# Strassen pairs of a feed-forward projection collected in running PSUM banks, with VectorE making the weight and column sums

## The chip, the cores and the metric

The kernel runs on one core of one Trainium2 chip. Its engines are TensorE (PE in the profile, its weight loads PEld), VectorE (DVE), ScalarE (ACT), GpSimd (POOL) and SyncE (SP), which only issues transfers here. The metric is the device time of one execution in microseconds; less is better. Compared are medians of runs of the kernel before and of the changed one.

## The reference, cut to what matters

One step of a decoder layer for a prompt of 512 tokens and eight samples of one token: 520 columns in all. The change touches the last part, behind the mixing of the two attention branches:

```python
mix = sigmoid(ga) * (oa @ w_pa) + sigmoid(gb) * (ob @ w_pb)
h = x + mix @ w_o
f = square(relu(rmsnorm(h, g_norm2) @ w_up))      # w_up: 1024 x 4096
y = rmsnorm(h + f @ w_down)                       # w_down: 4096 x 1024
```

All of it is float32. The outputs are `y`, the new key and value caches and the recurrent states.

## The kernel before

Activations lie transposed in SBUF: 128 features on the partitions, 520 columns along the row, in eight tiles `k` for the 1024 features. The columns fall in two halves of 260 (`HC`); `halves` shows a tile that way.

A float32 product is made of three matmuls, since operands are rounded to a shorter format (`F32R`): the rounded part is `hi`, the remainder `lo`, and the sum is hi x hi + hi x lo + lo x hi. Weights are split so on the chip: `split_piece` has ScalarE round a piece of 128 x 512 (`whi`, L107) and VectorE subtract (`wlo`, L108). `weight_tiles` gives the buffers, four of each kind in one pool and a fifth from a second pool.

Weights come in panels of 128 output features x 1024 input features. `self.panels` lists them in order: `w_in`, `w_pa`, `w_pb`, eight of `w_o`, and then four quarters (`qd`) of the feed-forward part, each with eight panels of `w_up` and eight of `w_down`. Panel `i+2` is loaded and panel `i+1` split while panel `i` is multiplied.

In the first three quarters the `w_up` panels run as four pairs (`PAIR`), by Strassen's scheme: seven products P1 to P7 of half size in place of eight. Each is a group of 12 matmuls (four input tiles, three passes) into 260 columns, so a pair has 84. `load_pair` loads the two panels and, with an accumulating transfer from GpSimd's queue (L96), the sums of their blocks (`sums`). `pair_pieces` yields the seven weight pieces, of which two (`s2`, `s4`) are sums that GpSimd adds (L124, L125). `column_sums` makes the matching sums of the activations (`hg`, the normalised `h` before the norm's factor) into `Th` and `Tl`. P1, P2 and P3 take `hh` and `hl`, the others `Th` and `Tl`. P6 needs the sums of the lower four tiles.

`pair_mm` runs the seven groups into three PSUM places: `a` and `b`, the two banks of a tile `m` (two such tiles), and `c`, a bank of its own (`self.pf`, four banks). `up_pair` combines them behind each group: ScalarE copies P1 and P5 out (L1092), VectorE adds (L1098, L1100, L1105, L1106, L1108), and ScalarE takes relu and square and rounds the result `f` to `fh`; VectorE makes `fl`. These are what the `w_down` panels read, whose results collect in `dd` (`panel_mm`, L225).

`H` is `h`; while `w_o` runs (L1296 on), VectorE adds its panels to `H` (L1298), ScalarE makes `hh` and `hg`, `column_sums` follows for the same tile, and the squares of `H` are added into `acc` for the norm. `spread` sums `acc` over the partitions on TensorE (L1317) and takes the reciprocal into `rv` (L1320); it stands behind the first pair. `rv` is used in the fourth quarter.

The order of an engine's instructions comes from a scheduler, which orders them by its own timing; `high_priority` moves a block ahead, `behind` forces an order without a wait, `after` adds a wait. In the pairs `behind` holds the matmuls of one pair in turn, but groups of different pairs and panels may interleave. Each engine then runs its list strictly in turn, waiting on semaphores.

GpSimd's queue also holds copies of the old caches from memory to memory (`pace`, L267), each held back until a certain matmul of `self.last` has run.

Of the kernel before, what the change touches and what calls it, by code (L numbers as in the profile page):

```python
# [9 lines left out]
F32 = mybir.dt.float32  # L10
# [37 lines left out]
class Build:  # L48
# [42 lines left out]
    def load_pair(self, i):  # L91

        ap, p = self.panels[i][0], self.late
        sums = p.tile([P, KT, P], F32, tag="sums", name="sums", bufs=2)
# [16 lines left out]
    def weight_tiles(self, n):  # L111
        self.nw += 1
        pool, bufs = (self.late, 1) if self.late is not None and self.nw % 5 == 0 else (self.wp, self.wbufs)
        return [pool.tile([P, n, P], F32R, tag=t, name=t, bufs=bufs) for t in ("whi", "wlo")]

    def pair_pieces(self, i):

        nc = self.nc
        ra, rb, sums = self.raw.pop(i)
        new = lambda: self.late.tile([P, 4, P], F32, tag="s", name="s", bufs=3)  # L120
        yield self.split_piece(ra, 0, 4)
        yield self.split_piece(sums, 4, 4)
        s2, s4 = new(), new()
        nc.gpsimd.tensor_tensor(s2, sums[:, 4:], ra[:, :4], op=ALU.add)  # L124
        nc.gpsimd.tensor_tensor(s4, s2, ra[:, 4:], op=ALU.add)  # L125
        order = {"12": lambda: self.split_piece(ra, 4, 4), "s2": lambda: self.split_piece(s2, 0, 4),
                 "s4": lambda: self.split_piece(s4, 0, 4), "s3": lambda: self.split_piece(sums, 0, 4),
                 "22": lambda: self.split_piece(rb, 0, 4)}
        for n in (("12", "s2") if i in self.first_pairs else ("s2", "12")) + ("s4", "s3", "22"):
            yield order[n]()  # L130
# [39 lines left out]
    def pair_mm(self, acts, done):  # L170
# [3 lines left out]
        m, c = self.pm.tile([P, 2, 512], F32, tag="m", name="mps"), self.bank("mps")  # L174
        a, b = m[:, 0, :HC], m[:, 1, :HC]
        c = c[:, :HC]
        mid = (("P2", a, False), ("P6", b, True)) if i in self.first_pairs else (("P6", b, True), ("P2", a, False))
        prev = None
        for q, (n, o, fresh) in enumerate((("P1", a, True), ("P5", c, True), *mid, ("P3", c, False), ("P7", b, False),
                                           ("P4", a, True))):  # L180
            with self.tc.high_priority():
                self.pieces_to(i, q + AHEAD)
            if q == 4 and i + 2 < len(self.panels):
                self.load_panel(i + 2)
            hi, lo = self.ready[i][q]
            for k in range(4):
                xh, xl = acts(n, k)
                for x, (w, u) in enumerate(((hi, xh), (hi, xl), (lo, xh))):
                    mm = nc.tensor.matmul(o, w[:, k], u, start=(fresh and k == 0 and x == 0), stop=(k == 3 and x == 2),  # L189
                                          skip_group_check=True)  # L190
# [29 lines left out]
    def k_tile(self, out, w, kw, k, xh, xl, kt):  # L220

        for j in range(2):
            o = out[j] if isinstance(out, list) else out[:, j]
            for n, (wt, x) in enumerate(self.passes(w, kw, xh, xl)):
                self.last = self.nc.tensor.matmul(o[:, :HC], wt, x[:, k, j * HC:(j + 1) * HC],  # L225
                                                  start=(k == 0 and n == 0), stop=(k == kt - 1 and n == 2))
# [831 lines left out]
    def column_sums(self, p, b, k, hi, lo):  # L1058
# [5 lines left out]
        if k < 4:  # L1064
            ts = slice(0, 1)
            nc.gpsimd.tensor_tensor(t[:, 0], b11, b12, op=ALU.subtract)
        else:
            ts = slice(1, 4)
            e = nc.vector if k == KT - 1 else nc.gpsimd
            e.tensor_tensor(t[:, 0], b22, b12, op=ALU.subtract)  # L1070
# [6 lines left out]
    def up_pair(self, p, work, k, fh, fl):  # L1077

        nc, tc, t, v = self.nc, self.tc, [work(), work()], {}
        new = lambda n: p.tile([P, HC], F32, tag=n, name=n, bufs=2)  # L1080
        one, two = slice(0, HC), slice(HC, NT)

        def split(x):
            nc.scalar.activation(t[x], t[x], AF.Square)
            nc.scalar.activation(fh[:, k + x], t[x], AF.Copy)
# [479 lines left out]
```

## Time and profile before

| | us |
|---|---|
| runs of the kernel before, median of 3 | 913.65 |
| lowest and highest of them | 912.48, 916.57 |
| the profiled execution's own time | 913.32 |
| its span, first to last instruction | 911.5 |
| matmuls of `w_o`, last panel ends | at 528.96 |
| first quarter with its pairs begins | at 530.24 |
| last matmul of the third quarter | at 808.56 |

A row of the trace's list in time has the start from the span's beginning, the length, engine, line, operation, the tile written and those read, and in brackets the idle time before it with what ended it. In grouped rows `x` is a count, then come busy time and the mean nanoseconds of one, then idle time ahead. TensorE's lengths overlap: a matmul of 260 columns is shown 0.28 us long, and starts follow each other faster than that.

### The profile page before, as it was taken

What the parts mean: (1) busy time and instruction counts of PE and PEld (TensorE: products, weight loads), DVE (VectorE), ACT (ScalarE), POOL (GpSimd) and SP (SyncE); (2) the same over time, 40 slices, a digit from 0 to 9 for tenths busy, and PEclk for the clock granted to TensorE, in tenths of its full rate; (3) what the DMA queues carried; (4) which work ended last, traced back from release to release, by engine and by line L of the source; (5) the groups of instructions that cost most, each with busy time, mean ns of one, the idle gap of its engine ahead of it and who ended that gap; (6) DMA issues with size and microseconds to landing.
All of it is one profiled execution on the core that took longest, in us unless ns stands there. A gap on an engine that the chain in (4) does not pass through costs nothing. (4 is left out here: it accounts for less than half of the span.)

```text
span 911.5 us, 19609 instructions
## 1 busy us (share of the span) xinstructions
PE 888.3 (97%) x8010; PEld 868.0 (95%) x8010; DVE 596.2 (65%) x1172; ACT 417.7 (46%) x844; POOL 128.9 (14%) x170
## 2 busy tenths in 40 slices
PE   9999999999999999999999969999999999999996
PEld 9999999999999999999999969999999989999996
DVE  6866666865867678676655588644863476656634
ACT  6334324454654454457334457623852466224342
POOL 1200000000111112010001433014301330000000
PEclk9999999999999999999999989999999999999998
DMA  7466455324534642222797966698869862222302
GB/s 252 155 239 210 131 202 204 117 73 157 196 132 151 213 148 91 76 72 72 279 318 274 290 221 195 231 339 295 244 232 353 254 224 94 102 92 90 136 9 86
DMA packets 42721, 165.16 MB, mean 181 GB/s; under 512 B 5692, under 2 KB 10820, under 8 KB 40808
## 3 DMA queue, kind: packets, MB, share of 16 engines
q1 hardware_dynamic: 33976, 97.93, 31.0%
q0 software_dynamic: 8368, 65.49, 21.5%
q8 instruction: 63, 1.03, 0.5%
q10 hardware_dynamic: 288, 0.49, 0.2%
q14 instruction: 26, 0.21, 0.1%
HBM read 150.17 MB, written 54.17 MB: 224 GB/s over the span
## 5 line engine op out<-in xcount | busy, mean ns | idle before, releaser
L107 ACT ACTIVATE whi<-raw 128x512 fp32r<-128x512 f32 (+1 forms) x242 | 149.3, 621 | 288.7 <-PE mps L225 237.6
L225 PE MATMUL mps<-uh,whi 128*128 128x260 f32 x896 | 255.8, 286 | 0.0
L225 PE MATMUL mps<-ul,whi 128*128 128x260 f32 x896 | 255.7, 285 | 0.0
L225 PE MATMUL mps<-uh,wlo 128*128 128x260 f32 x896 | 255.2, 285 | 0.0
L108 DVE TENSOR_TENSOR wlo<-raw,whi 128x512 fp32r<-128x512 f32 (+1 forms) x242 | 165.8, 689 | 70.2 <-ACT whi L107 68.4
L225 PEld LDWEIGHTS mps<-uh,wlo 128*128 128x128 f32 x896 | 168.7, 188 | 2.1 <-issue 1.5
L225 PEld LDWEIGHTS mps<-ul,whi 128*128 128x128 f32 x896 | 168.7, 188 | 1.2 <-issue 0.3
L225 PEld LDWEIGHTS mps<-uh,whi 128*128 128x128 f32 x896 | 168.7, 188 | 1.1 <-issue 0.7
L225 PE MATMUL mps<-fh,whi 128*128 128x260 f32 x384 | 108.6, 284 | 1.8 <-DVE t L1108 1.6
L225 PE MATMUL mps<-fh,wlo 128*128 128x260 f32 x384 | 108.4, 283 | 0.0
L225 PE MATMUL mps<-fl,whi 128*128 128x260 f32 x384 | 108.1, 282 | 0.0
L225 PEld LDWEIGHTS mps<-fh,whi 128*128 128x128 f32 x384 | 72.0, 188 | 3.0 <-DVE t L1108 2.2
L225 PEld LDWEIGHTS mps<-fh,wlo 128*128 128x128 f32 x384 | 72.3, 188 | 0.0
L225 PEld LDWEIGHTS mps<-fl,whi 128*128 128x128 f32 x384 | 72.2, 188 | 0.0
L189 PE MATMUL mps<-Th,wlo 128*128 128x260 f32 x192 | 53.4, 283 | 2.3 <-DVE wlo L108 2.3
L189 PE MATMUL mps<-Th,whi 128*128 128x260 f32 x192 | 54.4, 285 | 0.5 <-DVE P L1098 0.3
L189 PE MATMUL mps<-Tl,whi 128*128 128x260 f32 x192 | 53.9, 282 | 0.0
L189 PE MATMUL mps<-hh,whi 128*128 128x260 f32 x144 | 42.3, 294 | 8.8 <-ACT P L1092 6.1
L1380 PE MATMUL mps<-fh,lw 128*128 128x280 f32 (+1 forms) x256 | 46.8, 284 | 0.0
L189 PE MATMUL mps<-hl,whi 128*128 128x260 f32 x144 | 41.3, 287 | 0.0
L189 PE MATMUL mps<-hh,wlo 128*128 128x260 f32 x144 | 40.7, 286 | 0.0
L1380 PEld LDWEIGHTS mps<-fh,lw 128*128 128x128 f32 x256 | 39.7, 189 | 0.1
(383 smaller groups left out, 1966.1 us busy)
## 6 DMA issues: line engine op xcount, KB each, us to landing
raw<-in_w_in SPq DMA_DIRECT2D x55, 512.0 KB, 4.2
raw<-in_w_down SPq DMA_DIRECT2D x32, 512.0 KB, 4.5
raw<-in_w_up SPq DMA_DIRECT2D x20, 512.0 KB, 4.6
sums<-in_w_up SPq DMA_DIRECT2D x12, 512.0 KB, 4.6
sums<-in_w_up POOLq DMA_DIRECT2D x12, 512.0 KB, 8.6
sx<-in_state SPq DMA_DIRECT2D x8, 512.0 KB, 4.3
sx<-dV SPq DMA_DIRECT2D x8, 512.0 KB, 4.7
out_sgla<-sx POOLq DMA_DIRECT2D x8, 512.0 KB, 5.3
```

What stands on the lines that cost most here:

```text
L107: self.piece = (nc.scalar.activation(hi, raw[:, x:x + n], AF.Copy), nc.vector.tensor_tensor(lo, raw[:, x:x + n], hi.bitcast(F32), op=ALU.s ...
L108: nc.vector.tensor_tensor(lo, raw[:, x:x + n], hi.bitcast(F32), op=ALU.subtract))
L189: mm = nc.tensor.matmul(o, w[:, k], u, start=(fresh and k == 0 and x == 0), stop=(k == 3 and x == 2), skip_group_check=True)
L225: self.last = self.nc.tensor.matmul(o[:, :HC], wt, x[:, k, j * HC:(j + 1) * HC], start=(k == 0 and n == 0), stop=(k == kt - 1 and n == 2))
L1380: nc.tensor.matmul(ps, w, u[:, kk, cc], start=(kk == 0 and x == 0), stop=(kk == KT - 1 and x == 2))
```

## The change

The seven groups get a new order and new places. `x` is a bank of its own that runs through four of them, `a` and `e` are the two banks of a tile `ae`. P1 goes to `x`; ScalarE copies it from there to `a`. P5 goes to `e`; ScalarE copies it to SBUF. P6 is added in `x` on top of P1, and copied to SBUF. P3 is added in `e`, and VectorE adds P6 there. P7 is added in `x`; VectorE adds P5 to it. P2 is added in `a` on the copy of P1, and P4 in `x`. Two VectorE additions of 260 columns are left of five. `strict` keeps all matmuls from the feed-forward part on in program order, across pairs and panels.

`s2` and `s4` are now added by VectorE and rounded in one piece of 1024 columns. Pieces of 512 have four buffers, the wide one has one. `sums` has three buffers instead of two. The column sums run on VectorE and one tile behind. The squares of `H` move behind the `w_down` panels of the first quarter, and `spread` into those of the second.

```diff
-        sums = p.tile([P, KT, P], F32, tag="sums", name="sums", bufs=2)
+        sums = p.tile([P, KT, P], F32, tag="sums", name="sums", bufs=3)
...
     def weight_tiles(self, n):
-        self.nw += 1
-        pool, bufs = (self.late, 1) if self.late is not None and self.nw % 5 == 0 else (self.wp, self.wbufs)
-        return [pool.tile([P, n, P], F32R, tag=t, name=t, bufs=bufs) for t in ("whi", "wlo")]
+        pool, s, bufs = (self.wp, "", self.wbufs) if n <= 4 else (self.late, "2", 1)
+        return [pool.tile([P, n, P], F32R, tag=t + s, name=t, bufs=bufs) for t in ("whi", "wlo")]
...
         yield self.split_piece(sums, 4, 4)
-        s2, s4 = new(), new()
-        nc.gpsimd.tensor_tensor(s2, sums[:, 4:], ra[:, :4], op=ALU.add)
-        nc.gpsimd.tensor_tensor(s4, s2, ra[:, 4:], op=ALU.add)
...
-        for n in (("12", "s2") if i in self.first_pairs else ("s2", "12")) + ("s4", "s3", "22"):
-            yield order[n]()
+        s = self.late.tile([P, KT, P], F32, tag="s", name="s")
+        nc.vector.tensor_tensor(s[:, :4], sums[:, 4:], ra[:, :4], op=ALU.add)
+        nc.vector.tensor_tensor(s[:, 4:], s[:, :4], ra[:, 4:], op=ALU.add)
+        both = self.split_piece(s, 0, KT)
+        yield [t[:, :4] for t in both]
+        yield [t[:, 4:] for t in both]
+        yield self.split_piece(sums, 0, 4)
+        yield self.split_piece(ra, 4, 4)
+        yield self.split_piece(rb, 0, 4)
...
-        m, c = self.pm.tile([P, 2, 512], F32, tag="m", name="mps"), self.bank("mps")
-        a, b = m[:, 0, :HC], m[:, 1, :HC]
-        c = c[:, :HC]
-        mid = (("P2", a, False), ("P6", b, True)) if i in self.first_pairs else (("P6", b, True), ("P2", a, False))
-        prev = None
-        for q, (n, o, fresh) in enumerate((("P1", a, True), ("P5", c, True), *mid, ("P3", c, False), ("P7", b, False),
-                                           ("P4", a, True))):
+        ae, x = self.pm.tile([P, 2, 512], F32, tag="m", name="mps"), self.bank("mps")[:, :HC]
+        a, e = (ae[:, j, :HC] for j in range(2))
+        for q, (n, o, fresh) in enumerate((("P1", x, True), ("P5", e, True), ("P6", x, False), ("P3", e, False),
+                                           ("P7", x, False), ("P2", a, False), ("P4", x, False))):
             with self.tc.high_priority():
                 self.pieces_to(i, q + AHEAD)
-            if q == 4 and i + 2 < len(self.panels):
+            if q == 2 and i + 2 < len(self.panels):
                 self.load_panel(i + 2)
...
-                    if prev is not None:
-                        self.behind(mm, prev)
-                    prev = self.last = mm
-            done(n, o)
+                    self.behind(mm, self.last)
+                    self.last = mm
+            done(n, ae, x)
...
+                if self.strict:
+                    self.behind(mm, self.last)
+                self.last = mm
...
-            nc.gpsimd.tensor_tensor(t[:, 0], b11, b12, op=ALU.subtract)
+            nc.vector.tensor_tensor(t[:, 0], b11, b12, op=ALU.subtract)
         else:
             ts = slice(1, 4)
-            e = nc.vector if k == KT - 1 else nc.gpsimd
-            e.tensor_tensor(t[:, 0], b22, b12, op=ALU.subtract)
+            nc.vector.tensor_tensor(t[:, 0], b22, b12, op=ALU.subtract)
...
+        def keep(n, o):
+            v[n] = p.tile([P, HC], F32, tag=n, name=n)
+            nc.scalar.activation(v[n], o, AF.Copy)
+
+        def split(x, f):
+            nc.scalar.activation(fh[:, k + x], f, AF.Copy)
+            nc.vector.tensor_tensor(fl[:, k + x], f, fh[:, k + x].bitcast(F32), op=ALU.subtract)
...
+            if n == "P1":
                 with tc.high_priority():
-                    nc.scalar.activation(v[n], o, AF.Copy)
+                    nc.scalar.activation(a, x, AF.Copy)
+            elif n == "P5":
+                with tc.high_priority():
+                    keep(n, e)
+            elif n == "P6":
+                with tc.high_priority():
+                    keep(n, x)
+            elif n == "P3":
+                nc.vector.tensor_tensor(e, e, v["P6"], op=ALU.add)
+            elif n == "P7":
+                v["t"] = work()
+                with tc.high_priority():
+                    nc.vector.tensor_tensor(v["t"][:, two], x, v["P5"], op=ALU.add)
             elif n == "P2":
-                nc.scalar.activation(t[0][:, one], o, AF.Relu)
...
+                f = work()
+                nc.scalar.activation(halves(f), ae[:, :, :HC], AF.Relu)
+                nc.vector.tensor_tensor(f, f, f, op=ALU.mult)
+                split(0, f)
+                nc.scalar.activation(v["t"][:, two], v["t"][:, two], AF.Relu, scale=-1.0)
             else:
-                nc.vector.tensor_tensor(t[1][:, one], v["P7"], o, op=ALU.add)
-                nc.scalar.activation(t[1], t[1], AF.Relu, scale=-1.0)
-                split(1)
+                t = v["t"]
+                nc.scalar.activation(t[:, one], x, AF.Relu, scale=-1.0)
+                nc.scalar.activation(t, t, AF.Square)
+                split(1, t)
                 self.pace(1)
...
+                nc.vector.scalar_tensor_tensor(hl[:, k], H[:, k], self.g("n2", k), hh[:, k].bitcast(F32),
+                                               op0=ALU.mult, op1=ALU.subtract)
                 nc.scalar.activation(hg[:, k], H[:, k], AF.Copy, scale=self.g("n2", k))
-                nc.vector.tensor_tensor(hl[:, k], hg[:, k], hh[:, k].bitcast(F32), op=ALU.subtract)
-                self.column_sums(p, hg, k, Th, Tl)
...
+                if k > 0:
+                    self.column_sums(p, hg, k - 1, Th, Tl)
                 self.pace(1)
+            self.column_sums(p, hg, KT - 1, Th, Tl)
+            self.strict = True
...
-                        if qd == 0 and k == 0:
-                            spread()
...
+                        sq = work() if k else acc
+                        nc.scalar.activation(sq, H[:, k], AF.Square)
+                        if k:
+                            nc.vector.tensor_tensor(acc, acc, sq, op=ALU.add)
...
+                    if qd == 1 and k == 0:
+                        spread()
```

How the instructions stand before and after, at two places. First TensorE, in the second quarter, where the second pair's P1 ends; before (`mps_8313` is that pair's `a`, `mps_8314` its `c`, `mps_8165` the `a` of the pair ahead):

```order
L189 MATMUL mps_8313<-hl_6475,whi_8238 128x260
L189 MATMUL mps_8313<-hh_6474,wlo_8239 128x260
L189 MATMUL mps_8165<-Th_6477,whi_8203 128x260 [waits DVE_49]
L189 MATMUL mps_8165<-Tl_6478,whi_8203 128x260
L189 MATMUL mps_8165<-Th_6477,wlo_8204 128x260
```

The 12 matmuls of a group of the pair ahead stand there, and P5 follows only behind them. After (`mps_8259` is `x`, `mps_8258` the tile `ae` of the same pair):

```order
L185 MATMUL mps_8259<-hl_6475,whi_8194 128x260
L185 MATMUL mps_8259<-hh_6474,wlo_8195 128x260
L185 MATMUL mps_8258<-Th_6477,whi_8212 128x260 [waits Activation_49]
L185 MATMUL mps_8258<-Tl_6478,whi_8212 128x260
L185 MATMUL mps_8258<-Th_6477,wlo_8213 128x260 [waits DVE_49]
```

P5 now stands directly behind P1. Its first matmul waits for ScalarE (`Activation_49` is ScalarE's semaphore), and the value is the one that the copy of P1 into `a` reaches, the second-last row of the next piece.

ScalarE at the same place after the change, from the first pair's P6 copy to the second pair's P1 copy:

```order
L1081 ACTIVATE P6_8175<-mps_8120 128x260 [waits PE_49]
L107 ACTIVATE whi_8237<-s_8234 128x1024 [waits DVE_49,PE_49]
L107 ACTIVATE whi_8212<-sums_8043 128x512 [waits DMASW4_49,DMAHW6_49,DVE_49,PE_49]
L107 ACTIVATE whi_8273<-sums_8043 128x512 [waits DVE_49,PE_49]
L1109 ACTIVATE t_8210<-t_8210 128x260 [waits DVE_49]
L1106 ACTIVATE t_8228<-mps_8119 128x520 [waits PE_49]
L107 ACTIVATE whi_8291<-raw_8046 128x512 [waits PE_49]
L1112 ACTIVATE t_8210<-mps_8120 128x260 [waits PE_49]
L1113 ACTIVATE t_8210<-t_8210 128x520 [waits Activation_49]
L107 ACTIVATE whi_8316<-rb_8048 128x512 [waits DMAHW0_49,PE_49]
L1091 ACTIVATE mps_8258<-mps_8259 128x260 [waits PE_49]
L1084 ACTIVATE fh_7050<-t_8228 128x520 [waits DVE_49]
```

Before, P1's copy at this place stood behind the rounding of a piece of the next pair's `sums`, and no matmul of P5 waited for it:

```order
L1084 ACTIVATE t_8163<-t_8163 128x520 [waits Activation_49]
L107 ACTIVATE whi_8351<-sums_8089 128x512 [waits PE_49]
L1092 ACTIVATE P1_8331<-mps_8313 128x260 [waits PE_49]
L1085 ACTIVATE fh_7073<-t_8163 128x520 [waits Activation_49]
L107 ACTIVATE whi_8315<-raw_8092 128x512 [waits PE_49]
```

The copy moved behind the rounding of the same pair's last piece (`rb`), which waits for the eleventh matmul of P1, the last that reads the `whi` buffer it reuses.

More of the change, by code (lines that the diff above doesn't have):

```diff
@@ L119, in pair_pieces @@
         ra, rb, sums = self.raw.pop(i)
-        new = lambda: self.late.tile([P, 4, P], F32, tag="s", name="s", bufs=3)
         yield self.split_piece(ra, 0, 4)
         yield self.split_piece(sums, 4, 4)
-        s2, s4 = new(), new()
[L124 to L128, printed above, removed]
-        for n in (("12", "s2") if i in self.first_pairs else ("s2", "12")) + ("s4", "s3", "22"):
-            yield order[n]()
+        s = self.late.tile([P, KT, P], F32, tag="s", name="s")
[7 more added lines that the diff above has]
+        yield self.split_piece(rb, 0, 4)
     def pieces_to(self, i, n):
@@ L187, in pair_mm @@
                 xh, xl = acts(n, k)
-                for x, (w, u) in enumerate(((hi, xh), (hi, xl), (lo, xh))):
-                    mm = nc.tensor.matmul(o, w[:, k], u, start=(fresh and k == 0 and x == 0), stop=(k == 3 and x == 2),
+                for y, (w, u) in enumerate(((hi, xh), (hi, xl), (lo, xh))):
+                    mm = nc.tensor.matmul(o, w[:, k], u, start=(fresh and k == 0 and y == 0), stop=(k == 3 and y == 2),
                                           skip_group_check=True)
-                    if prev is not None:
-                        self.behind(mm, prev)
-                    prev = self.last = mm
-            done(n, o)
+                    self.behind(mm, self.last)
+                    self.last = mm
+            done(n, ae, x)
     def panel_mm(self, xh, xl, pool=None):
@@ L224, in k_tile @@
             for n, (wt, x) in enumerate(self.passes(w, kw, xh, xl)):
-                self.last = self.nc.tensor.matmul(o[:, :HC], wt, x[:, k, j * HC:(j + 1) * HC],
-                                                  start=(k == 0 and n == 0), stop=(k == kt - 1 and n == 2))
+                mm = self.nc.tensor.matmul(o[:, :HC], wt, x[:, k, j * HC:(j + 1) * HC],
+                                           start=(k == 0 and n == 0), stop=(k == kt - 1 and n == 2))
+                if self.strict:
+                    self.behind(mm, self.last)
+                self.last = mm
                 if self.cur == 3 and k == 6 and n + j == 0:
@@ L1077, in up_pair @@
     def up_pair(self, p, work, k, fh, fl):
-        nc, tc, t, v = self.nc, self.tc, [work(), work()], {}
-        new = lambda n: p.tile([P, HC], F32, tag=n, name=n, bufs=2)
+        nc, tc, v = self.nc, self.tc, {}
         one, two = slice(0, HC), slice(HC, NT)
-        def split(x):
-            nc.scalar.activation(t[x], t[x], AF.Square)
-            nc.scalar.activation(fh[:, k + x], t[x], AF.Copy)
-            nc.vector.tensor_tensor(fl[:, k + x], t[x], fh[:, k + x].bitcast(F32), op=ALU.subtract)
@@ L1116, in run @@
         pool = lambda n: tc.tile_pool(name=n, bufs=1)
-        self.last = None
+        self.last, self.strict = None, False
         order = []
-        self.first_pairs = set()
         ix = self.pidx
@@ L1133, in run @@
             if qd < 3:
-                self.first_pairs.add(len(order))
                 order += [(I["w_up"][qd * 8 + i:qd * 8 + i + 2], PAIR) for i in range(0, 8, 2)]
```

23 lines of the change are left out of this document (2 added, 21 removed).

## The prediction, as it was put on record before the changed kernel ran

> **What bounds the kernel now.** First comes the page, then busy time by stretch, then who TensorE (PE) waited for.
>
> ```profile
> span 911.5 us, 19609 instructions
> PE 888.3 (97%) x8010; PEld 868.0 (95%) x8010; DVE 596.2 (65%) x1172; ACT 417.7 (46%) x844; POOL 128.9 (14%) x170
> ```
>
> TensorE is busy for 97% of the span, so only its idle time and its speed can move the result. The stretches below are the 100 us before the feed-forward part, the three quarters in which pairs of panels run, and the start of the fourth quarter. Columns: length, PE busy with its count, granted clock, DMA share, GB/s.
>
> ```profile
> 429.10:529.00 99.90, 99.90 (x837) 1.00 0.84 285
> 529.00:808.60 279.60, 266.16 (x2167) 0.99 0.67 225
> 808.60:855.00 46.40, 46.40 (x389) 1.00 0.35 124
> ```
>
> Undisturbed, a matmul takes 99.90/837 = 0.119 us, and 46.40/389 says the same. At 0.1194 the 2167 of the middle stretch would need 258.7 us. They took 279.6, so **20.9 us are lost there**, and none before or behind it. No edit reaches outside this stretch and the projection just ahead of it. Who was waited for in it (total, times, longest):
>
> ```profile
> PE mps L189 <- ACT P L1092: 6.1, 1, 6.1
> PE mps L189 <- DVE wlo L108: 2.3, 2, 1.5
> PE mps L225 <- DVE t L1108: 1.6, 3, 0.5
> PE mps L189 <- ACT whi L107: 1.5, 3, 0.6
> PE mps L189 <- DVE H L1298: 1.0, 1, 1.0
> PE mps L189 <- DVE P L1098: 0.8, 3, 0.3
> ```
>
> The waits sum to 13.3 us; the rest is the end of the last matmul before each (0.28 us a matmul, started every 0.119), the slow first matmul behind each, and a slow clock after the longest. That one, in PE's rows of time (start, length):
>
> ```profile
> 533.08 0.28 PE L189 MATMUL mps<-Th,wlo 128*128 128x260 f32 x1
> 539.46 0.58 PE L189 MATMUL mps<-hh,whi 128*128 128x260 f32 x1 [6.09 <-ACT P L1092]
> 539.84 0.42 PE L189 MATMUL mps<-hl,whi 128*128 128x260 f32 x1
> 540.05 0.42 PE L189 MATMUL mps<-hh,wlo 128*128 128x260 f32 x1
> ...
> 542.22 1.94 PE L1317 MATMUL r<-acc,ones 128*128 128x260 f32 x4
> ```
>
> After the idle 6.09 us matmuls start every 0.215 us instead of 0.119. The cause lies upstream: VectorE waits for a difference of `hg` that GpSimd makes late, and ScalarE's copy `P` stands behind that work.
>
> ```profile
> 520.28 1.29 POOL L1070 TENSOR_TENSOR tr<-hg 128x260 f32<-128x260 f32 x1
> 521.61 0.43 DVE L1071 SCALAR_TENSOR_TENSOR tr<-tr,hg 128x260 f32<-128x260 f32 x1 [5.12 <-POOL tr L1070]
> ```
>
> **What goes.** Differences and sums leave GpSimd, so VectorE no longer waits 5.12 us here; the two `DVE wlo` stalls (2.3) hung on GpSimd's sums. I therefore take all 20.9 us as gone and count what the new order costs. VectorE's new work is not on PE's path by itself: two adds of 512 columns per pair take the place of two combinations of 260, and fit in its idle time.
>
> **What comes: P5 behind P1's copy.** In the new order P5's first matmul waits for ScalarE's copy of P1 (L1091), as the rows under the change show, and nothing of another pair stands between P1 and P5 any more. ScalarE has, directly ahead of that copy, the rounding of the pair's last weight piece into a buffer that P1's own eleventh matmul frees. The trace has this chain, behind another group:
>
> ```profile
> 632.29 0.28 PE L189 MATMUL mps<-hl,whi 128*128 128x260 f32 x1
> 632.42 0.28 PE L189 MATMUL mps<-hh,wlo 128*128 128x260 f32 x1
> 633.30 0.39 PE L189 MATMUL mps<-hh,whi 128*128 128x260 f32 x1 [0.60 <-ACT whi L107]
> 633.52 0.28 PE L189 MATMUL mps<-hl,whi 128*128 128x260 f32 x1
> 632.62 0.63 ACT L107 ACTIVATE whi<-raw 128x512 fp32r<-128x512 f32 x1 [0.53 <-PE mps L189]
> 633.15 0.37 ACT L1094 ACTIVATE t<-mps 128x260 f32<-128x260 f32 x1
> ```
>
> The rounding starts 0.33 after the eleventh matmul's start, the next ScalarE operation 0.53 later, and a read of 260 columns of PSUM takes 0.37; here PE started 0.05 after ScalarE's end. Put L1091 in the place of L1094: it ends at 633.52, PE starts at 633.57, 1.15 after the last matmul instead of 0.12. The first matmul behind a wait takes 0.22 (633.30 to 633.52) instead of 0.12. So a pair loses 1.03 + 0.10 = **1.13 us**. No row shows a ScalarE write into PSUM; I take 0.37, its read of PSUM with a write into SBUF. From SBUF to SBUF 260 columns take 0.41, so PSUM saves 0.04 on one side; it may save that on the other too (0.33) or cost it (0.41), which is 0.4 us either way over eleven pairs.
>
> ```profile
> L1092 ACT ACTIVATE P<-mps 128x260 f32<-128x260 f32 x24 | 8.9, 369 | 0.0
> L1101 ACT ACTIVATE t<-t 128x260 f32<-128x260 f32 x12 | 5.0, 413 | 2.7 <-DVE t L1100 2.7
> L1085 ACT ACTIVATE fh<-t 128x520 fp32r<-128x520 f32 x24 | 15.2, 634 | 0.3
> ```
>
> In the fourth pair of a quarter one rounding of `f` more (L1084 of the change; L1085 before, 0.63, 0.55 back to back) stands in that queue. From the start u of the previous pair's last matmul: rounding until u+0.73, relu +0.27, `f` +0.55, square +0.53, rounding +0.53, copy +0.37 gives u+3.0 where P5 could begin at u+1.55: 1.5 + 0.1 = 1.6. The first pair's copy is in the next term. So eight pairs at 1.13 and three at 1.6, 13.8 us; 0.3 more for the second pair, whose queue has `f` late too, and 0.5 less since the two row-sum matmuls (already among the 2167) now run inside one of these waits: **13.6 us**.
>
> **The handover.** P6 now comes third in every pair, and needs the column sums of the last tile of `h`, while P2, which needs less, moved to sixth. Durations of its chain:
>
> ```profile
> L1298 DVE TENSOR_TENSOR H<-mps,H 128x520 f32<-128x520 f32 x5 | 3.5, 691 | 0.8 <-PE mps L225 0.8
> L1299 ACT ACTIVATE hh<-H,gcols 128x520 fp32r<-128x520 f32 x5 | 3.6, 721 | 0.8 <-DVE H L1298 0.8
> L1300 ACT ACTIVATE hg<-H,gcols 128x520 f32<-128x520 f32 x5 | 3.6, 715 | 0.0
> L1070 DVE TENSOR_TENSOR tr<-hg 128x260 f32<-128x260 f32 x1 | 0.4, 423 | 0.0
> L1074 ACT ACTIVATE Th<-tr 128x780 fp32r<-128x780 f32 x4 | 3.4, 852 | 12.5 <-DVE tr L1072 12.5
> L1075 DVE TENSOR_TENSOR Tl<-tr,Th 128x780 fp32r<-128x780 f32 x4 | 3.9, 970 | 1.1 <-ACT Th L1074 1.1
> ```
>
> Zero is the start of the last `w_o` matmul. P1's eleventh starts at 1.3, so ScalarE rounds 1.6 to 2.2, copies to 2.5, makes `hh` to 3.2 and `hg` to 3.8 (each starts about 0.1 ahead of the one before it ending). VectorE makes the first difference 3.8 to 4.3 and the second to 4.6, is held by the seventh tile's `Tl` (ScalarE's `Th` to 4.6, 0.97 more) to 5.6, and makes the third difference to 5.9. `Th` of the eighth ends at 6.8, `Tl` at 7.8. P6's last two matmuls follow, and P3 starts at 8.1, where without waits it would at 4.4: **3.7 us**, P5's wait included. If the seventh tile's work is done earlier, 2.7; if VectorE arrives half an operation late at each of four steps, 4.7. All waits in it are under 1.1 us each.
>
> **Two smaller ones.** Just in the first pair VectorE has a 512-column add between the wide subtraction and the read of P7 that P4 waits for: ScalarE's wide rounding (1024 columns; from 0.63 at 512 and 0.85 at 780, 1.05) starts 0.2 after P3's last matmul, the subtraction (from 0.69 and 0.97, 1.23) ends at 2.5, the add at 3.1, the read at 3.5, where P4 could start at 3.0: 0.6 with the restart. In the other pairs the same sum without the add ends at 2.9, just in time. And eight squares for `acc`, moved into the first quarter's end, delay `fl` of the last tile by 0.6. Together **1.2 us**.
>
> ```profile
> L108 DVE TENSOR_TENSOR wlo<-s,whi 128x512 fp32r<-128x512 f32 x24 | 16.6, 693 | 4.9 <-ACT whi L107 4.9
> L107 ACT ACTIVATE whi<-s 128x512 fp32r<-128x512 f32 x24 | 15.0, 626 | 12.9 <-PE mps L225 6.8 <-PE mps L189 3.8 <-POOL s L125 2.2
> L1320 DVE RECIPROCAL rv<-rv 128x520 f32<-128x520 f32 x1 | 3.4, 3393 | 0.0
> ```
>
> The 3.39 us reciprocal moves with the row sums into the second quarter's fourth pair, where P5's long wait covers it: 0.
>
> **Sum:** 13.6 + 3.7 + 1.2 = 18.5 come, 20.9 go: 2.4 us less. The profiled execution took 913.3 us, 0.3 below the median of the runs, 913.65. So 910.9 by the profile, 911.3 by the median; I forecast **911.3**, and 908 to 915 if its steps hold (0.2 us either way in each of eleven waits, 1 us in the handover).
>
> **Rivals.** *The adds wait for memory* (slower). GpSimd's first add waited 38.9 us, ten times, for the accumulating transfer; now such waits stand in VectorE's queue, ahead of weight pieces and of the square that ScalarE needs.
>
> ```profile
> L124 POOL TENSOR_TENSOR s<-sums,raw 128x512 f32<-128x512 f32 x12 | 16.3, 1359 | 47.4 <-DMA sums<-in_w_up 38.9 <-DVE wlo L108 6.8 <-issue 1.7
> sums<-in_w_up POOLq DMA_DIRECT2D x12, 512.0 KB, 8.6
> DMA to landing us min/median/max: 3.1/8.3/11.3
> ```
>
> Against it: three `sums` buffers let the load go earlier. For it: in the second and third quarter the fourth pair's transfer stands in POOL's queue behind a copy held until the first pair ends. It issues 0.75 after that end and lands 8.6 to 11.3 later, at 9.4 to 12.1, where VectorE wants it at 10.1; ScalarE feels nothing until about 2 us after that. It decides from 12.1. If the third and fourth pairs of both quarters are held as GpSimd was, 3.9 each less 2, that is 8 us: 919.
>
> *The clock drops at the handover.* Its waits are short, but sum to 3.7 of some 8 us. If the granted clock halves as after 533.08, a stretch like the one quoted, with PE mostly busy, adds up to 3 us: 914.3.
>
> By the Trainium skill, "TensorE: Matmul & The Clock Gate", section "Part 1: The HAM clock gate", the clock halves after an idle window of about 3.4 us. The trace agrees for 6.09 us of idle time (0.215 against 0.119 us); by that rule no wait of this handover would halve it, and the sum stays.
>
> *P5 waits less.* If ScalarE's rounding is out of the way, the copy alone costs 0.28 + 0.05 + 0.37 + 0.05 - 0.12 + 0.10 = 0.73: eleven times 0.4 less, 907. If P5 does not wait at all, 13.6 less: 897.7. The copy writes one bank of the pair's tile and P5 the other, which speaks for it; the wait written in the program speaks against it, and decides.
>
> The Trainium skill, "PSUM — Partial Sum Buffer", section "PSUM bank collisions raise a hardware error", asks only that engines be kept apart within a bank; by that, P5 would need no wait for a write to the other bank, and the time would be that 897.7. No run here shows such a program.
>
> **How the numbers follow.** Forecast 0.50, adds held by memory 0.15, clock 0.15, shorter wait 0.15, no wait 0.05. Half a per cent, 4.6 us, is about what a measurement of this kernel can tell from no change: below 909.1 is faster, above 918.2 slower. Faster are the last two and a little of the forecast's edge, 0.22; slower is most of the first rival, 0.13; the same 0.65. The range, 906 to 919, takes in all but the no-wait case and the far ends.
>
> **What would show it.** TensorE's waits should be led by `mps <- ACT mps L1091`, about eleven to twelve times, each near 0.9 us of idle time. GpSimd should have no sums, VectorE no 5 us wait for it, and P6's waits at the handover should name `Th` and `Tl`. If L1091 is missing from the waits, or TensorE waits for a weight piece behind VectorE's add, the forecast is wrong.

## The result, and the profile after

Over 20 runs each the changed kernel takes 918.45 us (916.67 to 921.50), the kernel before 915.73 (912.48 to 918.47): a ratio of 1.0035, with a 95% interval of 1.0024 to 1.0046. It is a third of a per cent slower, and the forecast had 0.26% faster. The page of the changed kernel:

```profile
span 916.7 us, 19479 instructions
PE 889.3 (97%) x8010; PEld 868.3 (95%) x8010; DVE 595.0 (65%) x1167; ACT 412.8 (45%) x832; POOL 87.7 (10%) x139
```

GpSimd's busy time fell from 128.9 to 87.7 us, and TensorE is as busy as before: nothing of that reached the end. TensorE's waits in the changed kernel from 529 to 812 us, in the form of those before (total, times, longest):

```profile
PE mps L185 <- ACT mps L1091: 11.5, 12, 1.3
PE mps L185 <- ACT Th L1071: 4.0, 2, 3.6
PE mps L185 <- DVE Tl L1072: 1.6, 2, 1.2
PE mps L220 <- DVE fl L1085: 0.6, 1, 0.6
```

The first row is P5's wait for P1's copy, twelve times, as the order of the instructions had shown. The second is a wait that the forecast named, but with no part over 1.1 us; here one is 3.6 us, for `Th`. Where the loss lies is read from two stretches, the first 22 us behind the projection and the rest up to the fourth quarter (length, PE busy with its count, granted clock, DMA share, GB/s). The kernel before:

```profile
529.00:551.00 22.00, 14.63 (x95) 0.84 0.60 181
551.00:808.60 257.60, 251.53 (x2074) 1.00 0.67 228
```

And the change:

```profile
529.03:551.40 22.37, 15.79 (x96) 0.77 0.77 232
551.40:814.00 262.60, 251.37 (x2073) 1.00 0.64 218
```

Taking off 0.1194 us a matmul leaves what is lost. At the handover it was 22.00 - 95 x 0.1194 = 10.7 us, and is 22.37 - 96 x 0.1194 = 10.9. Behind it, it was 257.60 - 2074 x 0.1194 = 10.0, and is 262.60 - 2073 x 0.1194 = 15.1. Together 5.3 us more, against 5.2 by the two spans. So the pairs lose about what was forecast for them (13.6 and the smaller 1.2, 14.8 in all; 0.6 of it, the wait at the first pair's P4, belongs to the handover's stretch and did not come), and **nearly the whole error is the handover: 10.9 where 3.7 was forecast**. Its cause is in VectorE's rows of time (start, length, in brackets the idle time before with what ended it):

```profile
520.78 0.69 DVE L122 TENSOR_TENSOR s<-sums,raw 128x512 f32<-128x512 f32 x1 [3.51 <-DMA sums<-in_w_up]
521.39 0.69 DVE L1300 TENSOR_TENSOR H<-mps,H 128x520 f32<-128x520 f32 x1
...
531.41 0.69 DVE L122 TENSOR_TENSOR s<-sums,raw 128x512 f32<-128x512 f32 x1 [2.60 <-DMA sums<-in_w_up]
...
534.57 0.70 DVE L1300 TENSOR_TENSOR H<-mps,H 128x520 f32<-128x520 f32 x1
```

VectorE reaches the first pair's addition and stands 3.51 us for the accumulating transfer, then 2.60 us at the second pair's. Between the two it has no idle time. The last tile of `H` is read at 534.57, though the last matmul of `w_o` started at 528.75. ScalarE's `hh` and `hg` of that tile, its differences and `Th` come behind it, and the tile ahead of it is late too. TensorE in the same time:

```profile
528.75 0.28 PE L220 MATMUL mps<-mh,wlo 128*128 128x260 f32 x1
...
533.53 0.28 PE L185 MATMUL mps<-Th,wlo 128*128 128x260 f32 x1
537.44 0.58 PE L185 MATMUL mps<-Th,whi 128*128 128x260 f32 x1 [3.63 <-ACT Th L1071]
539.21 0.59 PE L185 MATMUL mps<-Tl,whi 128*128 128x260 f32 x1 [1.19 <-DVE Tl L1072]
...
542.04 0.42 PE L185 MATMUL mps<-hh,whi 128*128 128x260 f32 x1
542.26 0.42 PE L185 MATMUL mps<-hl,whi 128*128 128x260 f32 x1
```

At the end of these rows a matmul starts every 0.22 us instead of 0.12, with nothing waited for: the granted clock is 0.50 from 537.1 to 547.4.

VectorE stood for such transfers elsewhere too, and longer. Of the four waits that its list from 500 to 810 us puts down to them

```profile
DVE s L122 <- DMA sums<-in_w_up: 16.9, 4, 5.7
```

two are these; the other two, 5.71 and 5.07 us at the first pairs of the second and third quarter, fall into the `w_down` panels ahead, and TensorE waits for nothing there. In this kernel a hold cost TensorE time only where VectorE had none to make it up.

### The profile page after: what moved, and what is told of

It reads as the page before. It is cut to its first block, busy times and chain, and to the rows that moved or that the text cites. A ratio compares the mean times of both kernels' runs of the same rounds, so it can differ in the third digit from the quotient of the medians.

```text
span 916.7 us, 19479 instructions
## 1 busy us (share of the span) xinstructions
PE 889.3 (97%) x8010; PEld 868.3 (95%) x8010; DVE 595.0 (65%) x1167; ACT 412.8 (45%) x832; POOL 87.7 (10%) x139
## 4 chain that ended last, share of the span: by engine, by line
PE 90%; ACT 4%; DMA 3%; DVE 2%; issue 1%; SPq 0%; DVEq 0%; ACTq 0%; POOLq 0%
PE mps L220 64%; PE mps L185 10%; PE mps L1384 5%; DMA sums<-in_w_up 2%; ACT whi L107 1%; PE mps L384 1%; PE lev L813 1%; PE sps L559 1%; PE pvp L592 1%; PE gpo L922 1%; PE gpu L926 1%; PE ptp L576 1%; PE vps L523 1%; PE gpo L924 1%; PE gso L994 0%
## 5 line engine op out<-in xcount | busy, mean ns | idle before, releaser
L108 DVE TENSOR_TENSOR wlo<-raw,whi 128x512 fp32r<-128x512 f32 (+1 forms) x242 | 163.9, 680 | 75.5 <-ACT whi L107 73.2
L185 PE MATMUL mps<-Th,whi 128*128 128x260 f32 x192 | 56.7, 295 | 15.6 <-ACT mps L1091 11.5
L185 PEld LDWEIGHTS mps<-Th,whi 128*128 128x128 f32 x192 | 36.8, 192 | 18.7 <-ACT mps L1091 14.2
```

What stands on the lines that cost most here:

```text
L108: nc.vector.tensor_tensor(lo, raw[:, x:x + n], hi.bitcast(F32), op=ALU.subtract))
```

## Experiments

Each kernel was run beside the kernel before on the same chip. Ratios are to that, with 95% intervals. Not all rows come from one chip, so two rows are best compared by their ratios.

| kernel | median us | ratio |
|---|---|---|
| the change | 918.45 | 1.0035 (1.0024 to 1.0046) |
| before_diffs | 911.18 | 0.9955 (0.9941 to 0.9969) |
| before_diffs_adds | 920.76 | 1.0060 (1.0038 to 1.0081) |
| before_diffs_early | 911.63 | 0.9951 (0.9932 to 0.9970) |
| first_adds_gpsimd | 918.75 | 1.0028 (1.0010 to 1.0047) |
| copies_later | 918.84 | 1.0034 (1.0018 to 1.0051) |
| early_sums | 914.42 | 0.9992 (0.9976 to 1.0007) |
| own_banks | 917.21 | 1.0003 (0.9985 to 1.0021) |
| banks_pace | 913.70 | 0.9988 (0.9973 to 1.0002) |
| banks_pace_early | 910.45 | 0.9952 (0.9928 to 0.9977) |
| inplace_four | 902.00 | 0.9845 (0.9813 to 0.9877) |
| inplace_four_shared | 913.94 | 0.9985 (0.9973 to 0.9997) |
| inplace_four_pace | 902.32 | 0.9871 (0.9851 to 0.9891) |

### Parts of the change in the kernel before

before_diffs moves the differences of the column sums alone:

```diff
-            nc.gpsimd.tensor_tensor(t[:, 0], b11, b12, op=ALU.subtract)
+            nc.vector.tensor_tensor(t[:, 0], b11, b12, op=ALU.subtract)
...
-            e = nc.vector if k == KT - 1 else nc.gpsimd
-            e.tensor_tensor(t[:, 0], b22, b12, op=ALU.subtract)
+            nc.vector.tensor_tensor(t[:, 0], b22, b12, op=ALU.subtract)
```

> The kernel before with only one part of the change: the first difference of every column sum on VectorE instead of GpSimd. Theory (the 6.1 us wait at the handover and the half clock behind it came from VectorE waiting 5.1 us for GpSimd, whose queue was held by sums waiting for memory): TensorE's wait of 6.1 us falls under 2, the clock stays full, some 8 us less than before, 907 to 908 us. Rival (ScalarE and VectorE are late there for the work alone): a wait of 4 us or more stays, 913 to 916 us.

It took 911.18, 0.45% less than before. TensorE's longest wait at the handover, 6.1 us before, is now

```profile
PE mps L189 <- ACT P L1091: 1.8, 1, 1.8
```

and its clock there is full. The reading of the kernel before stands; the size is 4.1 us by the ratio, not the 8 expected. before_diffs_adds puts the two additions on VectorE as well:

```diff
-        nc.gpsimd.tensor_tensor(s2, sums[:, 4:], ra[:, :4], op=ALU.add)
-        nc.gpsimd.tensor_tensor(s4, s2, ra[:, 4:], op=ALU.add)
+        nc.vector.tensor_tensor(s2, sums[:, 4:], ra[:, :4], op=ALU.add)
+        nc.vector.tensor_tensor(s4, s2, ra[:, 4:], op=ALU.add)
```

> The kernel before with two parts of the change: the differences of the column sums and the two additions of each pair, all from GpSimd to VectorE; five combinations, its order and its buffers stay. Theory (an add on VectorE that waits for the accumulating transfer holds everything behind it there, while on GpSimd it held little): 3 to 8 us slower than with the differences alone (911.2 us), VectorE's list shows waits for the sums transfer of 10 us or more in all, TensorE's a wait over 3 us at the handover: 914 to 919 us. Rival (the adds cost only their work, and VectorE gains from GpSimd's silence, 0.69 for 1.25 us): 909 to 911 us.

920.76: by the two ratios 1.05% or **9.6 us more than with the differences alone**, for two additions a pair. VectorE's waits, its rows at the first pair, and TensorE's wait there:

```profile
DVE s L124 <- DMA sums<-in_w_up: 21.8, 9, 7.9
```

```profile
518.80 0.69 DVE L124 TENSOR_TENSOR s<-sums,raw 128x512 f32<-128x512 f32 x1 [7.88 <-DMA sums<-in_w_up]
...
520.35 0.69 DVE L1297 TENSOR_TENSOR H<-mps,H 128x520 f32<-128x520 f32 x1
```

```profile
PE mps L225 <- DVE H L1297: 3.2, 1, 3.2
```

One addition waits 7.88 us, the read of `H` stands behind it, and TensorE waits for that read already inside the projection. So one part of the change brings 4 us and the other takes more than that back. How much of the 9.6 us is waiting and how much work was not separated in this kernel.

### The hold at the handover, in the changed kernel

first_adds_gpsimd gives only the first two pairs' additions back to GpSimd:

```diff
-        nc.vector.tensor_tensor(s[:, :4], sums[:, 4:], ra[:, :4], op=ALU.add)
-        nc.vector.tensor_tensor(s[:, 4:], s[:, :4], ra[:, 4:], op=ALU.add)
+        self.npair = getattr(self, "npair", 0) + 1
+        eng = nc.gpsimd if self.npair <= 2 else nc.vector
+        eng.tensor_tensor(s[:, :4], sums[:, 4:], ra[:, :4], op=ALU.add)
+        eng.tensor_tensor(s[:, 4:], s[:, :4], ra[:, 4:], op=ALU.add)
```

> The changed kernel with the two additions of the first two pairs on GpSimd instead of VectorE; all others stay. Theory (VectorE's add, held 3.5 and 2.6 us by the accumulating transfer, delays the evacuation of the last projected tiles and so the column sums; its 3.6 us hole at TensorE halves the clock): the handover, about 11 us of lost time, falls to about the 3.7 us forecast, no wait of TensorE there over 1.3 us, clock full: 911 us. Rival (P6 in third place needs the last tile's column sums too early whatever VectorE does): the wait for the column sums stays near 3 us, 917 to 919 us.

918.75: nothing gained. The rival's number came, but not its mechanism. GpSimd's, ScalarE's and VectorE's rows of it:

```profile
520.39 1.23 POOL L96 DMA_DIRECT2D sums<-in_w_up  x1 [7.11 <-DMA sums<-in_w_up]
521.83 1.40 POOL L124 TENSOR_TENSOR s<-sums,raw 128x512 f32<-128x512 f32 x1 [0.22 <-DMA sums<-in_w_up]
```

```profile
525.07 1.06 ACT L107 ACTIVATE whi<-s 128x1024 fp32r<-128x1024 f32 x1 [3.71 <-POOL s L125]
```

```profile
526.16 1.22 DVE L108 TENSOR_TENSOR wlo<-s,whi 128x1024 fp32r<-128x1024 f32 x1 [2.64 <-ACT whi L107]
...
531.78 1.75 DVE L108 TENSOR_TENSOR wlo<-sums,whi 128x512 fp32r<-128x512 f32 x1
```

The transfers now hold GpSimd: it stands 7.11 us for the load of the second pair's `sums`, then 0.22 for the first pair's accumulation. Its additions hold the wide rounding on ScalarE, and that holds VectorE's subtraction. While GpSimd adds, a VectorE subtraction of 512 columns takes 1.75 us instead of 0.69. TensorE waited 6.5 us at P5. The hold has only changed its way to the same queue.

copies_later takes eight output copies out of the last projection's loop; they come later:

```diff
                     self.column_sums(p, hg, k - 1, Th, Tl)
-                self.pace(1)
```

> The changed kernel without the eight paced output copies of the last projection: they come behind, with the later ones. All on VectorE as in the change. Theory (the transfers of the first two pairs land late because the copies stand in GpSimd's queue and share the memory): they land some 3 us after issue sooner than the 10.8 and 7.8 us of the change, VectorE's first adds wait under 1 us, and the handover falls to about 4 us: 911 to 912 us. Rival (they are late by their own chain, a plain load, then the accumulation behind it, whatever else runs): VectorE still waits 2 to 3 us at the second pair, 917 to 919 us.

918.84. Without the copies the first two accumulations land in 8.9 and 6.2 us (10.8 and 7.8 in the change), but the scheduler puts the additions earlier as well:

```profile
516.42 0.69 DVE L122 TENSOR_TENSOR s<-sums,raw 128x512 f32<-128x512 f32 x1 [5.17 <-DMA sums<-in_w_up]
517.03 0.69 DVE L1300 TENSOR_TENSOR H<-mps,H 128x520 f32<-128x520 f32 x1
...
524.86 0.69 DVE L122 TENSOR_TENSOR s<-sums,raw 128x512 f32<-128x512 f32 x1 [0.91 <-DMA raw<-in_w_up]
...
528.63 0.69 DVE L1300 TENSOR_TENSOR H<-mps,H 128x520 f32<-128x520 f32 x1
```

The hold is 5.17 us, one tile earlier. From 516.42 to 538.05 VectorE is idle for 0.91 us and a few gaps of 0.04, so the delay isn't worked off: TensorE waited 5.3 us at P5. Neither expectation had this. It shows that at the handover VectorE has no slack in which to recover, wherever the hold comes.

early_sums takes the hold itself away. The sums transfers of the first two pairs are issued earlier, into buffers that are free by then (left out here are the lines that move a pair's load and accumulation into `load_sums`):

```diff
...
+                if k in (1, 3):
+                    n = self.cur + KT - (k + 1) // 2
+                    self.early[n] = self.load_sums(n)
                 ps = self.panel_mm(mh, ml)
```

> The changed kernel; only the sums transfers (load and accumulation) of the first two pairs are issued four and three panels earlier, in the second and fourth tile of the last projection. Theory (VectorE has work without a break in the last 15 us of the projection, so that any hold there, through the add or through a rounding behind it, comes out undiminished at the first pair): no VectorE wait for these transfers, the eighth tile of H is read under 2 us after its matmuls instead of 5.5, the handover costs 4 us instead of 11, the clock stays full: 911 us. Rival (VectorE's work alone is too much there): H still read 4 us late, 916 to 918 us.

914.42, by the ratios 0.43% or 3.9 us less than the change, about half of the gain expected. The last tile of `H` and the stretch of the handover:

```profile
529.69 0.69 DVE L1308 TENSOR_TENSOR H<-mps,H 128x520 f32<-128x520 f32 x1
```

```profile
529.30:551.30 22.00, 18.79 (x141) 0.92 0.86 275
```

VectorE reads `H` without a hold, and the handover loses 22.00 - 141 x 0.1194 = 5.2 us instead of 10.9, with the second pair's P5, 1.2, in it. So 6.9 of the 10.9 us go there when only these two transfers come earlier. Behind it the ten pairs left lose 257.50 - 2027 x 0.1194 = 15.5 us, where the eleven in the change lose 15.1; some 1.6 us are lost again there, 0.98 of them in a new wait in the second quarter. The clock still halves, for 3.4 us.

### P5's wait

own_banks puts `a` and `e` into two PSUM tiles; relu then takes one instruction for each half:

```diff
-        ae, x = self.pm.tile([P, 2, 512], F32, tag="m", name="mps"), self.bank("mps")[:, :HC]
-        a, e = (ae[:, j, :HC] for j in range(2))
+        a, e, x = self.pm.tile([P, 2, 512], F32, tag="m", name="mps")[:, 0, :HC], *(self.bank("mps")[:, :HC] for _ in range(2))
...
-                nc.scalar.activation(halves(f), ae[:, :, :HC], AF.Relu)
+                nc.scalar.activation(f[:, two], e, AF.Relu)
+                nc.scalar.activation(f[:, one], a, AF.Relu)
```

> The changed kernel, with the two sums that share one two-bank PSUM tile (P1's copy in bank a, P5 in bank e) put into two tiles. The program then writes no wait of P5 for the copy of P1; the copy must only end before P6, one group (1.43 us) later. Theory (the wait for the copy is a price of its own): the twelve waits for L1091, 12.4 us with restarts, go from TensorE's list; ScalarE has one more instruction (0.27 us) a pair, the fourth pairs may keep 0.2 us each before P6, so 906 to 907 us. Rival (the wait only moves, since ScalarE still rounds the last piece first): TensorE then waits at P6 or at a weight piece for about as long, 913 to 918 us.

917.21, by the ratios 0.32% or 2.9 us less than the change: all twelve waits at P5 are gone, but three others came. (The profiled run, 912.93, is the shortest of ten.)

```profile
PE mps L184 <- ACT mps L1089: 6.6, 3, 3.4
```

The three stand at P6, which goes on in the bank that the copy reads; two of them, 2.9 and 3.4 us, in the third pairs of the second and third quarter, while the fourth pair's pieces are made. In VectorE's and ScalarE's rows of the first of these:

```profile
648.13 0.69 DVE L122 TENSOR_TENSOR s<-sums,raw 128x512 f32<-128x512 f32 x1 [3.02 <-issue]
```

```profile
650.07 0.64 ACT L1083 ACTIVATE fh<-t 128x520 fp32r<-128x520 f32 x1 [2.92 <-DVE t L1106]
...
651.66 0.36 ACT L1089 ACTIVATE mps<-mps 128x260 f32<-128x260 f32 x1
```

This is the forecast's slower rival, in the place it named: the addition waits for the fourth pair's transfer (it landed at 648.05), the square behind it holds ScalarE, and P1's copy stands in that queue. In the change, where P5's waits make each pair some 1.2 us longer, VectorE waited 1.81 us at this addition, not 3.02, and TensorE did not wait for it. banks_pace also drops the output copy between pairs:

```diff
                 split(1, t)
-                self.pace(1)
```

> The kernel with two PSUM tiles for a and e (own_banks), and the paced output copy behind each pair left for later, so that the fourth pair's accumulation doesn't stand behind a copy that is held until the first pair ends. Theory (own_banks kept two waits of 2.9 and 3.4 us and a slow clock from the fourth pair's add, held by its transfer): these two go, 6 us in the profile and more in its slower runs: 908 to 911 us. Rival (these transfers are late by their length): the waits stay above 2 us, 915 to 918 us.

913.70, with an interval that overlaps that of own_banks. Waits of 2.9 and 1.5 us stay in the same two pairs, so the copy was not their main cause. banks_pace_early adds the earlier transfers of the first pairs, with the lines of early_sums:

> Both: own tiles for a and e without the copies between pairs, and the first two pairs' sums transfers earlier. Theory: no wait of TensorE over 1.5 us is left between the projection and the fourth quarter; of 26.7 us lost in the change some 5 to 7 remain: 898 to 901 us. Rival (VectorE's work holds the handover): 906 to 909 us.

910.45, short of the 898 to 901 expected. Waits of 2.7 and 2.3 us remain in the same two third pairs. The next expectation puts them down to the load of the fourth pair's `sums`, which would wait for a buffer that the quarter's first pair holds. inplace_four has a fourth buffer, and makes room for it:

```diff
-        sums = self.late.tile([P, KT, P], F32, tag="sums", name="sums", bufs=3)
+        sums = self.late.tile([P, KT, P], F32, tag="sums", name="sums", bufs=4)
...
-        pool, s, bufs = (self.wp, "", self.wbufs) if n <= 4 else (self.late, "2", 1)
-        return [pool.tile([P, n, P], F32R, tag=t + s, name=t, bufs=bufs) for t in ("whi", "wlo")]
+        self.nw += 1
+        pool, bufs = (self.late, 2) if self.late is not None and self.nw % 3 == 0 else (self.wp, self.wbufs)
+        return [pool.tile([P, n, P], F32R, tag=t, name=t, bufs=bufs) for t in ("whi", "wlo")]
...
-        s = self.late.tile([P, KT, P], F32, tag="s", name="s")
-        nc.vector.tensor_tensor(s[:, :4], sums[:, 4:], ra[:, :4], op=ALU.add)
-        nc.vector.tensor_tensor(s[:, 4:], s[:, :4], ra[:, 4:], op=ALU.add)
-        both = self.split_piece(s, 0, KT)
-        yield [t[:, :4] for t in both]
-        yield [t[:, 4:] for t in both]
+        nc.vector.tensor_tensor(sums[:, 4:], sums[:, 4:], ra[:, :4], op=ALU.add)
+        yield self.split_piece(sums, 4, 4)
+        nc.vector.tensor_tensor(ra[:, :4], sums[:, 4:], ra[:, 4:], op=ALU.add)
+        yield self.split_piece(ra, 0, 4)
```

> banks_pace_early, and a fourth buffer for the sums transfers; to make room for it the two additions are written over operands that are done with, and their results are rounded as two pieces of 512 instead of one of 1024. Theory (the 2.7 and 2.3 us waits that were left in the fourth pairs came from its load, which waits for a buffer that its quarter's first pair frees): the fourth pair's accumulation is issued 10 us earlier, these waits fall under 0.5 us, 6 us with their slow clock: 903 to 906 us. Rival (the memory is full there, 300 GB/s and more, so an earlier transfer only lands later or holds another): waits over 1.5 us stay, 908 to 911 us.

902.00, 1.55% less than the kernel before and, with the next but one, **the best of all**. It differs from banks_pace_early by the narrow pieces and their buffers too, and in the third quarter the trace does not credit the fourth buffer: the fourth pair's transfer lands 21.9 us behind the start of the quarter's first pair in both kernels (738.22 - 716.36 and 733.74 - 711.83). What differs is where the addition stands, one row for each kernel:

```profile
738.30 0.69 DVE L127 TENSOR_TENSOR s<-sums,raw 128x512 f32<-128x512 f32 x1 [2.38 <-issue]
```

```profile
738.72 0.68 DVE L127 TENSOR_TENSOR sums<-sums,raw 128x512 f32<-128x512 f32 x1
```

In banks_pace_early VectorE was ready for it at 735.92, 19.6 us behind that start and ahead of the landing. In inplace_four it comes at 26.9 us, behind the landing, and holds nothing. In the second quarter it comes at 26.9 us too, and there the transfer also lands earlier, at 16.2 us and not 23.3. Which of the edits moved the addition was not separated. VectorE's list has no wait for a transfer from 490 to 810 us, and TensorE's waits from 529 to 812 are

```profile
PE mps L188 <- ACT Th L1074: 1.7, 1, 1.7
PE mps L188 <- DVE t L1105: 1.0, 1, 1.0
PE mps L188 <- DVE Tl L1075: 0.4, 1, 0.4
PE mps L223 <- DVE fl L1088: 0.4, 1, 0.4
```

inplace_four_shared goes back to one tile for `a` and `e` in it, and nothing else:

> inplace_four with a and e again as the two banks of one PSUM tile, as in the change, so that the program writes P5's wait for the copy of P1; the transfers stay early. Theory (this wait has a price of its own, 12.4 us over the eleven later pairs in the change, also where no transfer is late): TensorE's list shows L1091's like in eleven waits near 0.9 us, 902 plus 11 to 13, 913 to 915 us. Rival (where VectorE and ScalarE are never held, the copy is early enough and the wait costs little): 903 to 906 us.

913.94, 11.9 us more, or 12.8 by the ratios. The stretch behind the handover without and with the shared tile, one row for each kernel:

```profile
551.90:798.50 246.60, 245.15 (x2032) 1.00 0.64 218
```

```profile
552.10:809.80 257.70, 245.70 (x2024) 1.00 0.61 208
```

246.60 - 2032 x 0.1194 = 4.0 us are lost in the one, 257.70 - 2024 x 0.1194 = 16.0 in the other. So P5's wait costs 12.0 us in the ten pairs that start in this stretch, 1.2 each. inplace_four_pace has the copies between pairs again, the line that banks_pace dropped:

> inplace_four with the paced output copy behind each pair as in the change. Theory (the fourth buffer and not the copies decided the fourth pairs' waits: in banks_pace they stayed without the copies): within 1.5 us of inplace_four, 901 to 904 us. Rival (the fourth pair's accumulation behind a copy that is held until the first pair ends is late again): waits over 2 us in the fourth pairs, 906 to 909 us.

902.32, the same as inplace_four within the intervals. Last, before_diffs with the lines of early_sums:

> The kernel before with the differences on VectorE and the first two pairs' sums transfers earlier; its sums stay on GpSimd, its five combinations and its order stay. Theory (with the additions on GpSimd the transfer holds little that TensorE waits for): within 2 us of the differences alone, 909 to 911.5 us; TensorE's 1.75 us wait at the handover stays over 1. Rival (the transfer holds the handover in this kernel too): the handover's waits go, 906 to 908 us.

911.63, the same as the differences alone. With the additions on GpSimd an earlier transfer brings nothing in all; in the profiled run TensorE's wait at the handover was even longer, 3.4 us.

## Why the prediction was wrong, point by point

**What goes.** "I therefore take all 20.9 us as gone" holds for the causes named: VectorE's list of waits in the change has none for GpSimd from 500 to 810 us, and of TensorE's six old waits none is left. before_diffs shows that the differences alone were worth 4.1 us.

**P5 behind P1's copy** was right in its cause, its count and its size: 14.8 us forecast with the two small terms, 15.1 measured behind the handover; by the pair of runs that differ in it alone 1.2 us a pair, where 13.6 us for eleven pairs were forecast. Of the small ones `fl` came, with 0.6 us of idle time; the wait at P4 did not. So the closeness of the two totals is in part luck.

**The failed step** is that VectorE's new work "is not on PE's path by itself" and fits "in its idle time", and with it the handover's sum, which began with a VectorE that was free when the last `w_o` matmul ran. The work was even under-counted: a square of 520 columns came to VectorE as well (L1107, 0.70 us), and three combinations went, not two. But its busy time hardly moved, 596.2 us before and 595.0 after. What the forecast put at nothing is the wait: an addition is 0.69 us of work, but it stands in the queue until its transfer has landed, and the read of `H` is queued behind it. The forecast knew that GpSimd's first addition had waited 38.9 us in all, and let such waits reach TensorE only in a rival, in the third and fourth pairs. In the change they cost TensorE time in the first two, with 3.51 and 2.60 us, where the pieces are made during the projection's last tiles and VectorE has no slack. The handover's own sum comes out about right once the hold is gone. In inplace_four_shared, which differs from the change in its pieces and copies too, where the clock stays full, its stretch and the second pair's P5 within it are

```profile
530.10:552.10 22.00, 17.96 (x143) 1.00 0.61 183
```

```profile
546.53 0.39 PE L189 MATMUL mps<-Th,whi 128*128 128x260 f32 x1 [1.29 <-ACT mps L1095]
```

22.00 - 143 x 0.1194 = 4.9 us, less about 1.5 for that wait with its restart leaves 3.4, where 3.7 was forecast. So the missing 7.2 us are the hold and the slow clock behind it; early_sums, which takes the hold alone away, wins 6.9 of them back in this stretch.

**The rivals.** *The adds wait for memory* was the right mechanism with the wrong place. Its 919 came within 0.6 us by luck, from another sum: at the fourth pair's addition in the second quarter VectorE did wait, 1.81 us, but TensorE did not wait for it. *The clock drops at the handover* came as well, and was counted apart from the first rival, though a longer hold brings both. *P5 waits less* did not come: its twelve waits are 0.96 us in the mean. *P5 does not wait at all* was no outcome of this program, but own_banks and inplace_four show that nothing but the shared tile asked for that wait. By the Trainium skill, "PSUM — Partial Sum Buffer", section "PSUM bank collisions raise a hardware error", engines are to be kept apart within one bank only; these runs agree, with the copy and P5 in two banks and no wait between them.

**The baseline.** The forecast went out from 913.65, the median of the three runs shown; over 20 runs it is 915.73. The profiled execution of before was one of the shorter ones, so 5.2 us by the spans are 2.7 by the medians; the sums by stretch here are those of the profiled executions.

## What to carry to other kernels

Price an operation that moves to another engine by the longest wait that it brings into that engine's queue, and by who stands behind it there: in the kernel before, two additions of 1.4 us of work a pair cost 9.6 us in all, and TensorE's first loss stands behind a wait of 7.88 us for a transfer. Look for such holds first where two stages overlap and the receiving engine has no idle time: there 3.51 and 2.60 us delayed TensorE, and 5.71 and 5.07 us elsewhere did not. The same addition placed later in the queue, behind the landing, holds nothing. A PSUM tile of two banks whose halves have different writers can write a wait into the program that two tiles don't have; here that was 12 us.

## What the runs showed of the hardware

The clock halved behind much less idle time than the 6.09 us of the kernel before. In inplace_four TensorE's longest is 1.74 us, and the clock fell before it was over:

```profile
536.13 0.59 PE L188 MATMUL mps<-Th,whi 128*128 128x260 f32 x1 [1.74 <-ACT Th L1074]
```

```profile
535.50:536.00 0.50, 0.00 (x0) 0.98 0.63 184
...
542.50:543.00 0.50, 0.50 (x4) 0.69 1.11 205
```

A share of 0.98 and one of 0.69 in windows of 0.5 us, with 0.50 in all between, put the half clock from 535.98 to 542.81, 6.8 us. In the same way it is 10.2 us in the change, 6.8 in the kernel before and 3.4 in early_sums: multiples of one length. In own_banks a wait of 2.94 us left the clock full, with a matmul every 0.12 us behind it:

```profile
652.08 0.39 PE L184 MATMUL mps<-Th,whi 128*128 128x260 f32 x1 [2.94 <-ACT mps L1089]
652.30 0.28 PE L184 MATMUL mps<-Tl,whi 128*128 128x260 f32 x1
652.42 0.28 PE L184 MATMUL mps<-Th,wlo 128*128 128x260 f32 x1
```

So the longest idle time alone does not decide; its place may. In own_banks the clock fell at 534.92 and at 743.13, 61 times 3.413 us (10.24 / 3) apart, and in banks_pace at 534.49 and 653.96, 35 times. Counted in such steps, the 2.94 us lie across a border, 1.8 ahead of it and 1.1 behind. This is a reading of the traces that no run was made to test. The prediction read the Trainium skill, "TensorE: Matmul & The Clock Gate", section "Part 1: The HAM clock gate", as asking for 3.4 us without a matmul; the 1.74 us contradict that reading. The same section calls the window free-running, which agrees with the multiples; how much idle time within one is enough, no run here shows.
